# Weight sums made by an adding transfer in six of twenty block-product pairs, with a new table of due times

## The chip, the cores and the metric

The kernel runs on one core of one Trainium2 chip. The metric is the device time of one execution in microseconds (us), as the median of several runs. A core has a matrix engine (TensorE, in the profile PE, with its weight loads shown apart as PEld), a vector engine (VectorE, DVE), a scalar engine (ScalarE, ACT), GpSimd (POOL) and SyncE (SP), which here only issues transfers; 16 DMA engines move the data.

## The reference, cut to what matters

Two decoder layers on 256 tokens of width 1024, float32 throughout. The two mixers differ (block-sparse attention, then a dilated window); after each comes the same MLP, and the change lies in the MLP's second product.

```python
SEQ, D_MODEL, D_FF, DEPTH = 256, 1024, 4096, 2

def sq_relu_mlp(x, w_in, w_out):
    return jnp.square(jax.nn.relu(x @ w_in)) @ w_out

for i in range(DEPTH):
    mix = moba_attention(...) if i % 2 == 0 else dilated_attention(...)
    h = layer_norm(DEEPNORM_ALPHA * h + mix, ...)
    h = layer_norm(DEEPNORM_ALPHA * h + sq_relu_mlp(h, w_in[i], w_out[i]), ...)
```

## The kernel before, in words

**Products.** Each float32 operand is split into a rounded part and a remainder, `hi` and `lo`, and each product is made as three matmuls: hi·hi, hi·lo and lo·hi. All matmuls are written in one helper, line L446 in the profile.

**Weights.** A weight piece of 128x1024 float32 (512 KB) is loaded by SP (L433) into one of 7 buffers named `raw`. ACT rounds it into `whi` (an ACTIVATE, L437), then DVE subtracts to make the remainder `wlo` (L442); `whi` and `wlo` have 10 buffers each, and PE reads them as weights. So each piece passes SP, DMA, ACT, DVE and PE in this order. DVE also copies and adds what comes out of PSUM (`ta`, `tok`, L788 and L795). `acc` and `tp` are PSUM banks.

**Pairs.** A large part of the second MLP product is made in a form of block product with seven multiplications in place of eight. A step of this kind ("pair" here, 10 to a layer, 20 in all) loads two 128x1024 pieces of `w_out`, x and y. With x0, x1 and y0, y1 for their halves of 512 columns, it needs seven weights of 512 columns: from x0 as loaded (w1), from y as loaded (w3, w2), then x0 += x1 and x1 += y0 and a split of the new x (w5, w7), then y0 += x0 and y1 += y0 and a split of the new y (w6, w4). The four sums are DVE tensor_tensor instructions of 128x512 (L788, `raw<-raw,raw` where two buffers or two keys differ, `raw<-raw` within one), 80 in all. `load_duo` writes a pair's loads, sums and splits; `q0` and `q1` are what the other operand becomes for a pair.

**What sets the order.** Nothing is written straight into the program: every operation goes into a planner (`Plan.op`) with its engine, an assumed cost, and what it reads and writes. `order()` gives each one a due time from PE's program order, adds the entry that the table `SHIFT` has for the operation's number, and then lists the operations of each engine by due time as far as buffers and inputs allow. `emit()` writes the program in that order. Each engine then runs its list in order, and waits on semaphores for what comes from others. So an entry of `SHIFT` can move instructions on every engine. SP's loads keep their own order.

**GpSimd** issues no transfer in the kernel before; it has the power step of the layer norm (`rstd`, L1043 and L1048) and a few small things. The adding transfer was already written in `load_duo`, behind a constant, `DMA_SUMS`, that was 0.

Of the kernel before, what the change touches and what calls it, by code (L numbers as in the profile page):

```python
# [12 lines left out]
ALU = mybir.AluOpType  # L13

P = 128
# [121 lines left out]
class Plan:  # L137
# [178 lines left out]
DMA_SUMS = 0.0  # L316
# [60 lines left out]
def tile_trunk(  # L377
# [22 lines left out]
    nc = tc.nc  # L400
    plan = Plan()
    op = plan.op
# [153 lines left out]
    for kt in range(KT):  # L556
        if kt % PER == 0:
            pair = [mk([P, 1024], F32R, t, NSLOT) for t in ("whi", "wlo")]
# [152 lines left out]
    def load_duo(pair, single):  # L711
# [16 lines left out]
        if DMA_SUMS:  # L728
            op(
                "POOL", DMA_SUMS, lambda: nc.gpsimd.dma_start(x.t, pair[:, 512:1536], accum_op=ALU.add), xk, xk,  # L730
                xfer=P * 1024 * 8,
            )
        else:
            tt(512, x0, x0, x1, ALU.add, xk, xk[:1])
            tt(512, x1, x1, y0, ALU.add, xk[1:] + yk[:1], xk[1:])
        w5, w7 = wide(x, 1)
        tt(512, y0, y0, x0, ALU.add, yk[:1] + xk[:1], yk[:1])
# [456 lines left out]
    class Mlp:  # L1194
# [17 lines left out]
        def rest(self, between):  # L1212
# [88 lines left out]
            def do_duo(p):  # L1301
# [4 lines left out]
                q = 1  # L1306
# [372 lines left out]
```

## Time and profile before

| | |
|---|---|
| runs, median (lowest to highest) | 546.93 us (546.81 to 547.24), 3 runs |
| profiled execution: span | 545.7 us, 8666 instructions |
| PE busy | 537.8 us, 3175 matmul records |
| DVE busy | 511.7 us |
| ACT busy | 362.2 us |
| POOL busy | 9.4 us |
| data moved | 105.62 MB, mean 194 GB/s |

The profiled execution has no time of its own beside the span: only the span of its instructions is known, 1.2 us below the median of the runs. The span starts with the first instruction on any engine and ends with the last. Layer 0's MLP lies at about 130 to 285 us, layer 1's at about 375 to 539 us; the pairs lie in both. A row of a table by windows gives the window's length and then, engine by engine, busy microseconds and in brackets the number of instructions; then the granted TensorE clock, the share of the DMA engines that was busy, and GB/s. A row of a timeline gives the start, the busy length, the engine, the line, the operation, output<-inputs and shapes. A row of the waits gives how long was waited in all, how many times, and the longest.

### The profile page before, as it was taken

What the parts mean: (1) busy time and instruction counts of PE and PEld (TensorE: products, weight loads), DVE (VectorE), ACT (ScalarE), POOL (GpSimd) and SP (SyncE); (2) the same over time, 40 slices, a digit from 0 to 9 for tenths busy, and PEclk for the clock granted to TensorE, in tenths of its full rate; (3) what the DMA queues carried; (4) which work ended last, traced back from release to release, by engine and by line L of the source; (5) the groups of instructions that cost most, each with busy time, mean ns of one, the idle gap of its engine ahead of it and who ended that gap; (6) DMA issues with size and microseconds to landing.
All of it is one profiled execution on the core that took longest, in us unless ns stands there. A gap on an engine that the chain in (4) does not pass through costs nothing.

```text
span 545.7 us, 8666 instructions
## 1 busy us (share of the span) xinstructions
PE 537.8 (99%) x3175; PEld 459.4 (84%) x3175; DVE 511.7 (94%) x885; ACT 362.2 (66%) x574; POOL 9.4 (2%) x15
## 2 busy tenths in 40 slices
PE   9999999999999999999999999999999999999994
PEld 7988888888888888888888888888888888888884
DVE  6798999798999999999999999988999999999997
ACT  6558798166958788864843549744877977865720
POOL 0000000000000000000000000000000000000001
PEclk9999999999999999999999999999999999999998
DMA  8985345528626562577845635444843855447502
GB/s 331 406 294 200 116 156 201 224 77 320 221 78 229 201 213 94 193 244 256 287 155 182 267 133 192 153 157 150 295 135 131 283 195 163 155 144 243 191 2 77
DMA packets 30282, 105.62 MB, mean 194 GB/s; under 512 B 3360, under 2 KB 4256, under 8 KB 30240
## 3 DMA queue, kind: packets, MB, share of 16 engines
q1 hardware_dynamic: 28800, 101.46, 53.4%
q10 hardware_dynamic: 1440, 3.61, 2.0%
q8 instruction: 25, 0.41, 0.3%
q14 instruction: 17, 0.14, 0.1%
HBM read 104.01 MB, written 1.05 MB: 193 GB/s over the span
## 4 chain that ended last, share of the span: by engine, by line
PE 84%; DVE 10%; issue 2%; ACT 2%; POOL 0%; DVEq 0%; ACTq 0%; POOLq 0%
PE acc L446 49%; PE tp L446 32%; DVE wlo L442 6%; PE tp L929 3%; DVE raw L788 2%; ACT whi L437 1%; DVE tok L795 1%; DVE ta L788 1%; DVE ta L442 0%; DVE tok L788 0%; POOL rstd L1043 0%; DVE ahi L442 0%; DVE bst L1101 0%; DVEq L1673 0%; ACT ta L1176 0%
## 5 line engine op out<-in xcount | busy, mean ns | idle before, releaser
L437 ACT ACTIVATE whi<-raw 128x1024 fp32r<-128x1024 f32 (+2 forms) x224 | 217.4, 1003 | 81.2 <-PE acc L446 31.2
L442 DVE TENSOR_TENSOR wlo<-raw,whi 128x1024 fp32r<-128x1024 f32 (+2 forms) x226 | 253.3, 1149 | 8.8 <-ACT whi L437 7.0
L446 PE MATMUL acc<-xs,whi 128*128 128x512 f32 (+1 forms) x464 | 107.8, 373 | 0.0
L446 PEld LDWEIGHTS acc<-xs,whi 128*128 128x128 f32 x464 | 81.1, 191 | 14.4 <-ACT xs L437 0.8
L446 PE MATMUL tp<-xs,whi 128*128 128x512 f32 x256 | 63.8, 392 | 0.0
L446 PEld LDWEIGHTS acc<-xs,wlo 128*128 128x128 f32 x416 | 56.9, 191 | 3.5
L446 PE MATMUL acc<-xs,wlo 128*128 128x256 f32 x416 | 59.8, 284 | 0.0
L446 PEld LDWEIGHTS tp<-xs,whi 128*128 128x128 f32 x256 | 46.8, 189 | 8.7
L446 PE MATMUL acc<-whi,ahi 128*128 128x512 f32 (+1 forms) x128 | 47.9, 391 | 0.0
L446 PE MATMUL acc<-wlo,ahi 128*128 128x512 f32 (+1 forms) x108 | 41.7, 386 | 0.0
L446 PEld LDWEIGHTS tp<-xs,wlo 128*128 128x128 f32 x256 | 34.7, 191 | 2.2
L446 PE MATMUL tp<-xs,wlo 128*128 128x256 f32 x256 | 35.6, 283 | 0.0
L446 PE MATMUL acc<-whi,alo 128*128 128x512 f32 (+1 forms) x92 | 33.8, 389 | 0.0
L446 PE MATMUL acc<-whi,xs 128*128 128x512 f32 (+1 forms) x112 | 29.1, 366 | 0.3 <-ACT xs L437 0.3
L788 DVE TENSOR_TENSOR raw<-raw 128x512 f32<-128x512 f32 x40 | 27.4, 688 | 0.6
L788 DVE TENSOR_TENSOR raw<-raw,raw 128x512 f32<-128x512 f32 x40 | 27.5, 688 | 0.5
L446 PEld LDWEIGHTS acc<-whi,ahi 128*128 128x128 f32 x128 | 24.0, 188 | 4.7 <-issue 0.3
L915 ACT ACTIVATE sc<-sc,mx 128x128 f32<-128x128 f32 (+2 forms) x40 | 19.9, 499 | 8.8 <-DVE mx L905 8.5
L446 PE MATMUL tp<-whi,xs 128*128 128x512 f32 x80 | 25.6, 398 | 0.0
L446 PEld LDWEIGHTS acc<-wlo,ahi 128*128 128x128 f32 x108 | 20.4, 188 | 3.7
L446 PEld LDWEIGHTS acc<-whi,xs 128*128 128x128 f32 x112 | 19.9, 189 | 3.8 <-ACT xs L437 0.5
L446 PEld LDWEIGHTS acc<-whi,alo 128*128 128x128 f32 x92 | 17.3, 188 | 3.6
(242 smaller groups left out, 887.0 us busy)
## 6 DMA issues: line engine op xcount, KB each, us to landing
raw<-in_win_dram SPq DMA_DIRECT2D x64, 512.0 KB, 4.3
raw<-in_wout_dram SPq DMA_DIRECT2D x64, 512.0 KB, 4.6
raw<-in_wqk_dram SPq DMA_DIRECT2D x22, 512.0 KB, 5.9
raw<-in_wo_dram SPq DMA_DIRECT2D x14, 512.0 KB, 4.4
raw<-in_wv_dram SPq DMA_DIRECT2D x8, 512.0 KB, 5.6
raw<-in_wv1a_dram SPq DMA_DIRECT2D x4, 512.0 KB, 4.7
tok<-in_xw_dram SPq DMA_DIRECT2D x2, 512.0 KB, 7.1
tok<-in_x_dram SPq DMA_DIRECT2D x2, 512.0 KB, 5.6
```

The source lines that it names most:

```text
L437: op("ACT", act(n, sbuf=sbuf), lambda: nc.scalar.activation(hi(), src(), AF.Copy), r, whi)
L442: lambda: nc.vector.tensor_tensor(lo(), src(), f32(hi()), op=ALU.subtract), list(r) + list(whi), wlo,
L446: nc.tensor.matmul(out_ap, lhsT, rhs, start=start, stop=stop)
L788: op("DVE", dve(n) + extra, lambda: nc.vector.tensor_tensor(out_ap(), a(), b(), op=alu), r, w)
L795: lambda: nc.vector.scalar_tensor_tensor(dst(), a(), s(), b(), op0=o0, op1=o1), r, w,
L915: lambda: nc.scalar.activation(e(), e(), AF.Exp, bias=bias(), scale=-1.0, accum_out=total()), r, w,
L929: nc.tensor.transpose(ps.t[:, c : c + P], src(), ident.t)
```

## The change

In three pairs of each layer (those with index 1, 4 and 7 in the order in which the layer makes them) the two sums x0 += x1 and x1 += y0 are no longer DVE instructions. One transfer that GpSimd issues reads the columns 512 to 1535 of the pair's weights from device memory again, which are x1 and y0 as loaded, and adds them onto x (512 KB read, 128x1024). It must wait until x has landed and both ACT and DVE have read x0 for w1; the split of the new x must wait until it has landed. In layer 1's pair with index 4 the sum y0 += x0 is an adding transfer too, from SBUF to SBUF (256 KB), that must wait for the first one. The table `SHIFT` is replaced as a whole: some 300 entries before, an entry for nearly every operation now. The scratch space for software-built transfers is doubled.

```diff
-DMA_SUMS = 0.0
+DMA_SUMS = 1.0
+ADDED = ({1: 1, 4: 1, 7: 1}, {1: 1, 4: 2, 7: 1})
...
 SHIFT = {
-    178: 5.0, 197: 7.4, 222: 6.2, 229: 27.3, 237: 5.8, 268: -10.9, 276: 15.7, 279: 19.0, 288: 10.5, 308: 29.9, 311:
...
+    0: 1.4, 1: 0.9, 2: -30.7, 3: -23.6, 4: -0.8, 6: -6.8, 8: -4.5, 9: -6.5, 10: -9.7, 11: -6.6, 12: -20.5, 13: 5.8,
...
-    def load_duo(pair, single):
+    def load_duo(pair, single, added):
...
         w3, w2 = wide(y, 0)
-        if DMA_SUMS:
+        if added:
             op(
                 "POOL", DMA_SUMS, lambda: nc.gpsimd.dma_start(x.t, pair[:, 512:1536], accum_op=ALU.add), xk, xk,
                 xfer=P * 1024 * 8,
             )
         else:
             tt(512, x0, x0, x1, ALU.add, xk, xk[:1])
             tt(512, x1, x1, y0, ALU.add, xk[1:] + yk[:1], xk[1:])
         w5, w7 = wide(x, 1)
-        tt(512, y0, y0, x0, ALU.add, yk[:1] + xk[:1], yk[:1])
+        if added == 2:
+            op(
+                "POOL", DMA_SUMS, lambda: nc.gpsimd.dma_start(y0(), x0(), accum_op=ALU.add), yk[:1] + xk[:1], yk[:1],
+                xfer=P * 512 * 8,
+            )
+        else:
+            tt(512, y0, y0, x0, ALU.add, yk[:1] + xk[:1], yk[:1])
         tt(512, y1, y1, y0, ALU.add, yk, yk[1:])
         w6, w4 = wide(y, 2)
...
-                w1, w2, w3, w4, w5, w6, w7 = load_duo(wout[i][p], (*single[0], q))
+                w1, w2, w3, w4, w5, w6, w7 = load_duo(wout[i][p], (*single[0], q), ADDED[i].get(sum(x[0] in 'sS' for x in steps) - 1 - left[0], 0))
...
-    nc = _bacc.Bacc("TRN2", target_bir_lowering=False, num_devices=1, dynamic_dma_scratch_size=256)
+    nc = _bacc.Bacc("TRN2", target_bir_lowering=False, num_devices=1, dynamic_dma_scratch_size=512)
```

Every line number behind the table moves with its new length: L433, L437, L442, L446 and L788 become L718, L722, L727, L731 and L1079; the adding transfers are L1015 and L1024.

How the order moves. PE, ACT and SP have the same instructions as before, DVE has 13 sums fewer, POOL 7 transfers more. SP's list keeps its order. Of PE's some 3130 listed instructions about 2380 stand at another place, by up to 118 places; on DVE the shift reaches 70 places, on ACT 31. The layer norms at the very end stand as before.

The first place is DVE at layer 0's pair with index 4, which lies at about 205 us in the trace of before. x is `raw_503`, y is `raw_504`; w1's remainder goes to `wlo_502`, those of w3/w2, w5/w7 and w6/w4 to `wlo_506`, `wlo_508` and `wlo_510`; `ta`, `g` and `b` rows and `raw_518` belong to other work. Before:

```order
L442 TENSOR_TENSOR wlo_502_2483<-raw_503_2320,whi_501_2469 128x512
L788 TENSOR_TENSOR ta_446_2492<-ta_445_2485 128x256
L788 TENSOR_TENSOR raw_503_2320<-raw_503_2320 128x512
L788 TENSOR_TENSOR raw_503_2320<-raw_503_2320,raw_504_2329 128x512
L442 TENSOR_TENSOR wlo_506_2504<-raw_504_2329,whi_505_2490 128x1024
L788 TENSOR_TENSOR raw_504_2329<-raw_504_2329,raw_503_2320 128x512
L442 TENSOR_TENSOR wlo_508_2524<-raw_503_2320,whi_507_2511 128x1024
L788 TENSOR_TENSOR ta_446_2492<-ta_455_2522 128x256
L788 TENSOR_TENSOR raw_504_2329<-raw_504_2329 128x512
```

After, from the row behind `wlo_502` on:

```order
L1079 TENSOR_TENSOR raw_518_2411<-raw_518_2411 128x512
L1079 TENSOR_TENSOR ta_429_2385<-ta_421_2325,ta_429_2385 128x128
L1079 TENSOR_TENSOR raw_518_2411<-raw_518_2411,raw_519_2451 128x512
L727 TENSOR_TENSOR b_423_2505<-ta_429_2385,b_423_2505 128x384
L1079 TENSOR_TENSOR ta_446_2489<-ta_455_2521 128x256
L727 TENSOR_TENSOR wlo_506_2527<-raw_504_2346,whi_505_2510 128x1024
L1079 TENSOR_TENSOR ta_456_2538<-ta_446_2489 128x128
L1079 TENSOR_TENSOR ta_446_2489<-ta_446_2489 128x128
L1079 TENSOR_TENSOR ta_456_2538<-ta_446_2489,ta_456_2538 128x128 x2
L727 TENSOR_TENSOR q0lo_448_2554<-ta_446_2489,q0hi_447_2547 128x512
L727 TENSOR_TENSOR q1lo_450_2561<-ta_456_2538,q1hi_449_2550 128x384
L1079 TENSOR_TENSOR raw_504_2346<-raw_504_2346,raw_503_2315 128x512
```

The two sums into `raw_503` are gone, and between w1's remainder and the first row that reads the transfer's result, the sum into `raw_504` at the end, now lie twelve instructions (one row stands for two); behind it come the other sum of `raw_504`, a `ta` row of 128x256, and `wlo_508` and `wlo_510`.

On PE at the same pair, where w5 and w7 (`whi_507`, `wlo_508`) are used first. Before, counted from the program's first matmul, the last two rows are its 1377th and 1378th:

```order
L446 MATMUL acc_284_2150<-whi_509_2545,q0lo_448_2580 128x512
L446 MATMUL acc_481_2636<-xs0_1_74,whi_483_2355 128x512 x4
L446 MATMUL acc_481_2636<-xs1_2_75,whi_483_2355 128x512 x4
L446 MATMUL acc_481_2636<-xs0_1_74,wlo_484_2367 128x256 x4
L446 MATMUL acc_481_2636<-xs1_2_75,wlo_484_2367 128x256 x4
L446 MATMUL tp_384_2188<-whi_507_2511,q0hi_447_2570 128x512
L446 MATMUL tp_384_2188<-wlo_508_2524,q0hi_447_2570 128x512
```

After:

```order
L731 MATMUL acc_475_2585<-xs0_1_74,whi_477_2333 128x512
L731 MATMUL acc_475_2585<-xs1_2_75,whi_477_2333 128x512 x2
L731 MATMUL tp_384_2124<-whi_507_2567,q0hi_447_2547 128x512
L731 MATMUL tp_384_2124<-wlo_508_2583,q0hi_447_2547 128x512
L731 MATMUL tp_384_2124<-whi_507_2567,q0lo_448_2554 128x512
L731 MATMUL acc_284_2160<-whi_509_2581,q0hi_447_2547 128x512
L731 MATMUL acc_284_2160<-wlo_510_2594,q0hi_447_2547 128x512
```

The first matmul with `whi_507` (the third row) is the 1348th of the program now, and the first with `wlo_508` the 1349th, 29 places ahead of where they stood; the weights made from y's sums (`whi_509`) now follow, where they came ahead.

The second place is DVE at layer 1's pair with index 4, the one with two transfers: x is `raw_1040`, y is `raw_1041`, and the remainders are `wlo_1039` (w1), `wlo_1043`, `wlo_1045` (w5, w7) and `wlo_1047` (w6, w4). Before:

```order
L442 TENSOR_TENSOR wlo_1039_5191<-raw_1040_5025,whi_1038_5186 128x512
L788 TENSOR_TENSOR ta_983_5199<-ta_982_5179 128x256
L788 TENSOR_TENSOR raw_1040_5025<-raw_1040_5025 128x512
L442 TENSOR_TENSOR wlo_1043_5208<-raw_1041_5035,whi_1042_5193 128x1024
L788 TENSOR_TENSOR raw_1040_5025<-raw_1040_5025,raw_1041_5035 128x512
L788 TENSOR_TENSOR raw_1041_5035<-raw_1041_5035,raw_1040_5025 128x512
L788 TENSOR_TENSOR ta_983_5199<-ta_992_5223 128x256
L788 TENSOR_TENSOR raw_1041_5035<-raw_1041_5035 128x512
L442 TENSOR_TENSOR wlo_1045_5240<-raw_1040_5025,whi_1044_5229 128x1024
L788 TENSOR_TENSOR ta_993_5251<-ta_983_5199 128x128
L788 TENSOR_TENSOR ta_993_5251<-ta_983_5199,ta_993_5251 128x128
```

After, from the fifteenth row behind w1's remainder on:

```order
L1079 TENSOR_TENSOR ta_983_5208<-ta_992_5232 128x256
L727 TENSOR_TENSOR wlo_1045_5249<-raw_1040_5031,whi_1044_5240 128x1024
L1079 TENSOR_TENSOR ta_993_5260<-ta_983_5208 128x128
L1079 TENSOR_TENSOR ta_993_5260<-ta_983_5208,ta_993_5260 128x128
L1079 TENSOR_TENSOR ta_983_5208<-ta_983_5208 128x128
L1079 TENSOR_TENSOR ta_993_5260<-ta_983_5208,ta_993_5260 128x128
L1079 TENSOR_TENSOR ta_999_5273<-ta_998_5266 128x256
L727 TENSOR_TENSOR q0lo_985_5281<-ta_983_5208,q0hi_984_5269 128x512
L1079 TENSOR_TENSOR raw_1041_5046<-raw_1041_5046 128x512
L727 TENSOR_TENSOR q1lo_987_5291<-ta_993_5260,q1hi_986_5278 128x384
L727 TENSOR_TENSOR wlo_1047_5303<-raw_1041_5046,whi_1046_5293 128x1024
L727 TENSOR_TENSOR wlo_1051_5311<-raw_1049_5060,whi_1050_5301 128x1024
```

Three of the four sums are gone, and the whole group, which stood in fourteen rows, is drawn out over 26: w1's remainder stands fifteen rows earlier in DVE's list than before (eight of the fifteen because pairs ahead of it make eight sums fewer), and w6/w4's remainder, `wlo_1047`, is first used by the program's 2807th matmul, where the first was the 2806th before.

The third place is POOL from layer 0's mixer norm to the last mixer norm. Before:

```order
L1048 TENSOR_TENSOR rstd_254_67<-rstd_254_67,expo_3_100 128x1
L1048 TENSOR_TENSOR rstd_276_1529<-rstd_276_1529,expo_3_100 128x1
L1048 TENSOR_TENSOR rstd_611_3190<-rstd_611_3190,expo_3_100 128x1
L1048 TENSOR_TENSOR rstd_630_3235<-rstd_630_3235,expo_3_100 128x1
L1048 TENSOR_TENSOR rstd_791_4173<-rstd_791_4173,expo_3_100 128x1
L1048 TENSOR_TENSOR rstd_813_4230<-rstd_813_4230,expo_3_100 128x1
L1048 TENSOR_TENSOR rstd_1146_5863<-rstd_1146_5863,expo_3_100 128x1
```

After:

```order
L1339 TENSOR_TENSOR rstd_276_1523<-rstd_276_1523,expo_3_100 128x1
L1015 DMA raw_403_1752<-in_wout_dram 128x1024
L1015 DMA raw_503_2315<-in_wout_dram 128x1024
L1015 DMA raw_542_2629<-in_wout_dram 128x1024
L1339 TENSOR_TENSOR rstd_611_3182<-rstd_611_3182,expo_3_100 128x1
L1339 TENSOR_TENSOR rstd_630_3232<-rstd_630_3232,expo_3_100 128x1
L1339 TENSOR_TENSOR rstd_791_4170<-rstd_791_4170,expo_3_100 128x1
L1339 TENSOR_TENSOR rstd_813_4232<-rstd_813_4232,expo_3_100 128x1
L1015 DMA raw_940_4493<-in_wout_dram 128x1024
L1015 DMA raw_1040_5031<-in_wout_dram 128x1024
L1024 DMA raw_1041_5046<-raw_1040_5031 128x512
L1015 DMA raw_1079_5337<-in_wout_dram 128x1024
```

Three transfers stand ahead of layer 0's MLP norm, four ahead of layer 1's; nothing else lies between them on POOL.

342 rows, old and new, of the table SHIFT are left out of this document.

## The prediction

> **What bounds the kernel now.** I read the busy times first, then the chain that ended last, then busy time by stretches, then what PE waited for.
>
> ```profile
> span 545.7 us, 8666 instructions
> PE 537.8 (99%) x3175; PEld 459.4 (84%) x3175; DVE 511.7 (94%) x885; ACT 362.2 (66%) x574; POOL 9.4 (2%) x15
> PE 84%; DVE 10%; issue 2%; ACT 2%; POOL 0%; DVEq 0%; ACTq 0%; POOLq 0%
> ```
>
> PE is busy 99% of the span, DVE 94%, and the chain runs 84% through PE and 10% through DVE. Two engines are thus near full, and the average can't tell which of them holds the other. The stretches can (window, then busy time of PE, PEld, DVE, ACT, POOL):
>
> ```profile
> 0.00:30.00 30.00, 29.23 (x194) 25.97 (x195) 22.25 (x41) 18.99 (x30) 0.94 (x6) 1.00 0.94 363
> 130.00:206.00 76.00, 76.00 (x418) 66.21 (x417) 72.38 (x115) 59.96 (x92) 0.00 (x0) 1.00 0.59 200
> 206.00:285.00 79.00, 79.00 (x372) 66.23 (x371) 78.63 (x116) 53.12 (x68) 0.99 (x1) 1.00 0.62 210
> 285.00:375.00 90.00, 89.75 (x641) 76.71 (x640) 84.52 (x166) 51.81 (x88) 2.76 (x3) 1.00 0.46 166
> 440.00:539.00 99.00, 98.85 (x491) 83.74 (x489) 97.00 (x147) 60.84 (x80) 0.92 (x1) 1.00 0.45 150
> 539.00:545.70 6.70, 0.00 (x0) 0.00 (x0) 3.60 (x7) 0.40 (x1) 1.77 (x2) 0.71 0.23 78
> ```
>
> In the later halves of the two MLPs (206 to 285 and 440 to 539 us) DVE idles 0.37 us of 79 and 2.0 of 99: there it runs level with PE. Yet PE lost nothing in the first and 0.15 us in the second; DVE works off a stock of ready weights and never empties it. Besides these, PE idles 0.77 us at the start and 0.25 at 285, and 6.7 us at the end belong to the last norm, which no row of the change touches. PE's own waits:
>
> ```profile
> PE tp L446 <- PEq L1664: 0.8, 1, 0.8
> PE acc L446 <- ACT xs L437: 0.3, 1, 0.3
> 285.45 0.50 PE L446 MATMUL acc<-whi,xs 128*128 128x512 f32 x1 [0.25 <-ACT xs L437]
> PEld L446 <- issue: 2.4, 7, 0.7
> PEld acc L446 <- ACT xs L437: 1.3, 2, 0.8
> PEld tp L446 <- ACT whi L437: 0.7, 2, 0.4
> ```
>
> One is the program's start, the other lies between the layers. The weight loads' rows below them matter because a matmul's end is modelled: up to 1.3 + 0.7 = 2.0 us of real waiting on ACT may hide in "busy". So PE is the bound nearly throughout, and what it can win by better feeding is 0.4 us visibly and about 2 us at most.
>
> **The change part by part.** PE has the same matmuls in the same shapes: 0 us.
>
> DVE loses 13 sums, seven written `raw<-raw,raw` and six `raw<-raw`:
>
> ```profile
> L788 DVE TENSOR_TENSOR raw<-raw,raw 128x512 f32<-128x512 f32 x40 | 27.5, 688 | 0.5
> L788 DVE TENSOR_TENSOR raw<-raw 128x512 f32<-128x512 f32 x40 | 27.4, 688 | 0.6
> L442 DVE TENSOR_TENSOR wlo<-raw,whi 128x1024 fp32r<-128x1024 f32 x198 | 236.0, 1220 | 8.0 <-ACT whi L437 6.4 <-PE acc L446 0.6
> L437 ACT ACTIVATE whi<-raw 128x1024 fp32r<-128x1024 f32 x198 | 202.8, 1055 | 79.0 <-PE acc L446 30.8 <-DVE raw L788 15.3 <-DVE tok L795 13.5
> ```
>
> 13 x 0.688 = 8.9 us, 4.1 in layer 0 and 4.8 in layer 1. It lies beside PE's matmuls, so its direct worth is only the wait at 285 us, behind the stretch in which DVE was full: -0.25 us, between 0 and -0.5 (that row's whole matmul).
>
> POOL gets seven transfers. None is in the trace of before; the nearest rows are plain loads of the same size, the slowest of that size, and POOL's own arithmetic:
>
> ```profile
> raw<-in_wout_dram SPq DMA_DIRECT2D x64, 512.0 KB, 4.6
> tok<-in_xw_dram SPq DMA_DIRECT2D x2, 512.0 KB, 7.1
> raw<-in_xw_dram SPq DMA_DIRECT2D x3, 256.0 KB, 5.0
> q1 hardware_dynamic: 28800, 101.46, 53.4%
> L1048 POOL TENSOR_TENSOR rstd<-rstd,expo 128x1 f32<-128x1 f32 x7 | 6.6, 950 | 524.7 <-DVE rstd L1046 524.7
> ```
>
> A load of the same bytes lands in 4.6 us: the lower bound, since adding must read x as well. Twice the slowest, 14.2 us, is the upper one. Between them I build an estimate: queue 1 moved 101.46 MB in 53.4% of 545.7 us, so 512 KB cost 291 / 101.46 x 0.524 = 1.5 us of all 16 engines; reading x too costs about that once more, and POOL's making of the transfer about one POOL instruction, 0.95 us. 4.6 + 1.5 + 0.95 = 7.1 us. The 256 KB one I take at its plain row, 5.0 us, since device memory isn't in it.
>
> Where does 7.1 us decide anything? The narrowest single place is layer 0's pair with index 4.
>
> ```profile
> 205.20 0.69 DVE L442 TENSOR_TENSOR wlo<-raw,whi 128x512 fp32r<-128x512 f32 x1
> 206.14 0.68 DVE L788 TENSOR_TENSOR raw<-raw 128x512 f32<-128x512 f32 x1
> 206.86 0.69 DVE L788 TENSOR_TENSOR raw<-raw,raw 128x512 f32<-128x512 f32 x1
> 217.34 0.40 PE L446 MATMUL tp<-whi,q0hi 128*128 128x512 f32 x1
> 222.85 0.40 PE L446 MATMUL tp<-whi,q0hi 128*128 128x512 f32 x1
> ```
>
> w1's remainder ends at 205.89 and may release the transfer; the two sums began 0.25 us later. w5 was used at 222.85. In the new list its remainder meets the program's 1349th matmul, which ran at 217.34 before. Behind the landing DVE has two sums, a 128x256 row (0.42) and the remainder: 2 x 0.69 + 0.42 + 1.22 = 3.0 us. So landing may take 217.34 - 205.89 - 3.0 = 8.4 us (if release and PE keep their distance to one another): 7.1 fits with 1.3 to spare. DVE has twelve instructions to run meanwhile, by their shapes some 6 us, and would then idle 1 us: covered by the two sums that it saved.
>
> The second place is layer 1's pair with index 4, where two transfers follow each other.
>
> ```profile
> 458.70 1.96 DVE L442 TENSOR_TENSOR wlo<-raw,whi 128x1024 fp32r<-128x1024 f32 x2 [0.20 <-ACT whi L437]
> 472.88 0.39 PE L446 MATMUL acc<-whi,q0hi 128*128 128x512 f32 x1
> 473.34 0.39 PE L446 MATMUL acc<-whi,q0lo 128*128 128x512 f32 x1
> ```
>
> w1's remainder (the second of the pair of rows) ended at 460.66. The last weights, `wlo_1047`, now meet the 2807th matmul, at 473.34 in the trace of before. Behind the second landing come one sum, ACT's rounding and the remainder, 0.69 + 1.06 + 1.22 = 3.0 us; that leaves 473.34 - 460.66 - 3.0 = 9.7 us if the release stays where it was. It comes earlier: seven of its fifteen rows are real reordering, at 97.00 / 147 = 0.66 us a row 4.6 us, so up to 14.3 us. The two transfers need 7.1 + 5.0 = 12.1, about the middle of these bounds. I take 0, with +2.4 us as the other end.
>
> The other four pairs have 12 to 22 rows of DVE between release and first reader, 8 to 14 us at 0.66 a row: wide enough at 7.1. The norm on POOL behind each group of transfers stands tens of microseconds after them: 0. SP's list keeps its order, but x keeps its buffer until the split behind the landing, some 6 us longer, and the loads that want one of the seven buffers come later; seven buffers of 512 KB at 210 GB/s turn over in 17 us, so one held 6 us longer delays one load by less than the stock covers: 0 to +1, I take 0. The added traffic, 6.5 x 0.524 = 3.4 MB on 105.6, falls where 45 to 62% of the DMA engines' time is used.
>
> Last the table. About 2380 of 3130 PE rows move. The matmuls cost the same anywhere; what can change is whether each weight and each emptied PSUM bank is there in time. The list after has more places where a remainder stands close ahead of its matmul, and in the stretches from 206 and 440 us a few more than before. One such wait costs 0.3 to 0.4 us by the rows of PE and PEld above; I take one or two, +0.5, between -2.0 (all hidden waits on ACT go) and +2.
>
> Sum on the profiled execution: 545.7 - 0.25 + 0.5 = 545.95, that is no change that matters. The median of the runs lies 1.2 us above that span, and with the same 1.2 the time is 547.1.
>
> **The rivals.** Late transfers (slower): if adding takes not 7.1 but 10 us, layer 0's narrow pair is 1.6 us late on PE, and layer 1's chain 10 + 5 - 12 = 3 us, where 12 is the middle of its two bounds; the rest stay hidden: 547.1 + 4.6 = about 551.5. At the upper bound of 14.2 us it is 5.8 + 7.2 us from these two and a microsecond or two from the other layers' pairs: about 561. It decides from 8.4 + 1.1 = 9.5 us on. For it speaks that no adding transfer was seen and that DMA is 62% busy there; against it, that most loads of the size land in 4.6 us under that same load.
>
> Held-off transfers (slower): DVE is full in just these stretches, and if POOL can build a transfer only while DVE pauses, it is built when DVE stops at the first reader, after some 6 us; then it lands at 6 + 7.1 = 13 us, 4.7 us too late at layer 0's pair, and 3 to 5 us at each of three others: 560 or so. In the trace POOL's rows in DVE's full stretches are only single norms of about 0.95 us, and none shows a stretched one. The Trainium skill ("SBUF — State Buffer", Who interferes with whom) has a rule of this kind: transfers from GpSimd starve while DVE runs in a two-port mode, and two SBUF inputs hamper only a GpSimd instruction that reads. DVE's rows here are mostly of the two-input kind, so by the page's exact wording this rival is unlikely, and no run yet shows it.
>
> Just-in-time order (slower): +0.3 to 0.4 at five or six of the new tight places instead of one or two, 548.5 to 549.
>
> Better feeding (faster): the relief of 8.9 us refills the stock in the two full stretches, and PE loses neither the 0.25 us at 285 nor the hidden waits on ACT: 546.93 - 0.25 - 2.0 = 544.7. Against it: the stock never ran out before.
>
> The sums hidden anyway, nothing else moved: 546.9, which my forecast can't be told from.
>
> **How the numbers follow.** No difference under 0.2%, 1.1 us here, can be told. No measurable change: 0.44, at 547.1 with 546.0 to 548.0 as its own range. Late transfers: 0.20. Held off: 0.06. Just-in-time: 0.12. Better feeding: 0.18, of which nearly all lies between 544.7 and 545.8. So faster 0.18, same 0.44, slower 0.38. The range leaves out the far half of the late transfers and the held-off case above (0.13) and a little of the fast case below (0.06): 545.2 to 551.5.
>
> **What would show it.** Right: PE at 537 to 539 us busy, no PE wait on whi or ta above 1 us, DVE's busy time down to about 503, the adding transfers landing 6 to 8 us from issue, the last norm still 6.7 us long. Wrong: landings above 9.5 us with DVE idle ahead of `raw<-raw,raw` or ACT ahead of `whi` on the transfer, and PE gaps near 217 or 472 us; gaps elsewhere would be the table's; a shorter PE stretch from the first matmul to the last with no transfer late would be better feeding.

## The result: 0.5% slower, and the profile after

| | before | after |
|---|---|---|
| median of the runs | 547.09 us (546.81 to 547.61, 4 runs) | 550.18 us (549.89 to 550.46, 4 runs) |
| ratio after to before | | 1.0053, 95% interval 1.0038 to 1.0067 |
| profiled execution: span | 545.7 us | 548.2 us (time 550.44) |
| start of the last matmul | 538.57 us | 540.49 us |

One execution of the kernel before (1387 us, beside e1 to e4) and one of e4 (782 us) lie far outside all others and are left out of every ratio.

The page of the changed kernel, its first lines and its list of waits on PE:

```profile
span 548.2 us, 8686 instructions
PE 539.0 (98%) x3175; PEld 458.3 (84%) x3175; DVE 505.8 (92%) x872; ACT 362.4 (66%) x574; POOL 15.0 (3%) x22
PE 90%; DVE 6%; DMA 2%; issue 1%; ACT 0%; DVEq 0%; SPq 0%; POOL 0%
```

```profile
PE tp L731 <- PEq L1955: 0.8, 1, 0.8
PE acc L731 <- ACT ta L1555: 0.7, 1, 0.7
PE tp L1220 <- DVE tok L1086: 0.2, 1, 0.2
```

PE is the bound as before: the chain runs 90% through it, and DVE got lighter. The old wait at 285 us on ACT's `xs` is gone; a wait on ACT's `ta` has come, 0.7 us, on the matmuls of L731 that write `acc`. The stretches say where (columns as in the prediction):

```profile
206.00:285.00 79.00, 79.00 (x370) 65.94 (x368) 77.03 (x113) 52.24 (x67) 2.78 (x3) 1.00 0.69 223
440.00:541.00 101.00, 100.08 (x497) 84.53 (x495) 95.31 (x145) 61.39 (x81) 3.57 (x4) 1.00 0.51 154
541.00:548.20 7.20, 0.00 (x0) 0.00 (x0) 3.52 (x7) 0.40 (x1) 1.01 (x2) 0.76 0.40 146
```

DVE's idle time grew in both of its full stretches, from 0.37 us to 1.97 of 79, and from 2.0 of 99 to 5.7 of 101. PE made nothing of it: in the last stretch it idles 0.92 us where it idled 0.15. This is the timeline there, in layer 1's pair with index 4:

```profile
466.81 1.98 PE L731 MATMUL acc<-xs,whi 128*128 128x512 f32 x8
468.62 1.11 PE L731 MATMUL acc<-xs,wlo 128*128 128x256 f32 x8
469.77 0.60 ACT L1555 ACTIVATE ta<-acc 128x512 f32<-128x512 f32 x1 [1.42 <-PE acc L731]
470.42 0.97 PE L731 MATMUL acc<-xs,whi 128*128 128x512 f32 x3 [0.69 <-ACT ta L1555]
```

Three of the four `acc` banks hold running sums of the MLP's second product here; one, the working bank, is left to make the other operand, product after product (988, 994, 1012 in the list). The 16 matmuls of product 994 end at 469.7, ACT empties the bank until 470.4, and only then can 1012 begin. Before, six matmuls on other banks stood between these two products, the first and the last of them in the two middle rows here (1012 begins in the last row); in the new list there are none.

```profile
465.82 1.00 PE L446 MATMUL acc<-xs,wlo 128*128 128x256 f32 x7
466.66 0.40 PE L446 MATMUL tp<-whi,sc 128*128 128x512 f32 x1
467.82 0.39 PE L446 MATMUL acc<-whi,v 128*128 128x512 f32 x1
468.05 1.98 PE L446 MATMUL acc<-xs,whi 128*128 128x512 f32 x8
```

The transfers did what was asked of them (start, busy time, engine, operation; in brackets POOL's idle time and what ended it):

```profile
207.83 0.90 POOL L1015 DMA_DIRECT2D raw<-in_wout_dram  x1 [53.14 <-DVE raw L1079]
458.51 0.88 POOL L1015 DMA_DIRECT2D raw<-in_wout_dram  x1 [51.51 <-DVE wlo L727]
466.45 0.89 POOL L1024 DMA_DIRECT2D raw<-raw  x1 [7.06 <-DMA raw<-in_wout_dram]
raw<-in_wout_dram SPq DMA_DIRECT2D x64, 512.0 KB, 4.9
raw<-in_wout_dram POOLq DMA_DIRECT2D x6, 512.0 KB, 5.7
raw<-raw POOLq DMA_DIRECT2D x1, 256.0 KB, 3.2
```

0.9 us on POOL, and 5.7 us from issue to landing, in which the POOL row is counted; the small one 3.2 us. One by one, four of the six landed in 5.5 to 5.7 us and two, of layer 1, in 7.1 and 7.3.

Put together, the last matmul starts 1.92 us later. Part of that is the start of the execution: in e11 (below) PE has the same list as in the changed kernel, yet its traced execution is 0.7 us ahead from 13 us on and stays so to the last matmul, 539.78 against 540.49. The last group of norm transposes of layer 0's mixer (PE's rows `tp<-ident,tok` at 118.7 us before and 119.1 after) is a mark behind which this no longer counts. From the mark to the last matmul PE takes 419.85 to 419.88 us in three traces with the old list (before, e2, e9) and 421.39 to 421.46 in three with the new one (after, e11, e6): 1.5 us more. Against each shape's usual pitch, PE lost 0.95 us of it at 469 us (the 0.69 of the row and the slow restart behind it); the other 0.6 us is spread, 0.3 of it over the stretch from the mark to 292 us. The stretch from the last matmul to the end of the span is 0.58 us longer (6.85 and 7.43 us), and the time lies 2.2 us above the span, where the kernel before lies 1.8 above it (its executions beside the experiments with the least change, below). 1.92 + 0.58 + 0.45 = 2.95 us is what lies between these two executions; the medians are 3.1 us apart.

### The profile page after: what moved, and what is told of

It reads as the page before. It is cut to its first block, busy times and chain, and to the rows that moved or that the text cites. A ratio compares the mean times of both kernels' runs of the same rounds, so it can differ in the third digit from the quotient of the medians.

```text
span 548.2 us, 8686 instructions
## 1 busy us (share of the span) xinstructions
PE 539.0 (98%) x3175; PEld 458.3 (84%) x3175; DVE 505.8 (92%) x872; ACT 362.4 (66%) x574; POOL 15.0 (3%) x22
## 4 chain that ended last, share of the span: by engine, by line
PE 90%; DVE 6%; DMA 2%; issue 1%; ACT 0%; DVEq 0%; SPq 0%; POOL 0%
PE acc L731 54%; PE tp L731 34%; PE tp L1220 3%; DVE tok L1086 2%; DVE wlo L727 2%; DMA g<-in_xw_dram 1%; DMA raw<-in_xw_dram 1%; DVE bst L1392 0%; DVE ta L727 0%; DVE tok L1079 0%; DVE bst L1362 0%; ACT whi L722 0%; DVE ta L1079 0%; ACT ta L1555 0%; DVE mv L1332 0%
## 5 line engine op out<-in xcount | busy, mean ns | idle before, releaser
L722 ACT ACTIVATE whi<-raw 128x1024 fp32r<-128x1024 f32 (+2 forms) x224 | 217.5, 1003 | 83.4 <-PE acc L731 24.0
L727 DVE TENSOR_TENSOR wlo<-raw,whi 128x1024 fp32r<-128x1024 f32 (+2 forms) x226 | 252.2, 1147 | 7.8 <-ACT whi L722 6.4
L731 PE MATMUL acc<-xs,whi 128*128 128x512 f32 (+1 forms) x464 | 110.7, 372 | 0.8 <-ACT ta L1555 0.7
L731 PEld LDWEIGHTS acc<-xs,whi 128*128 128x128 f32 x464 | 81.1, 190 | 15.7 <-ACT ta L1555 0.9
L731 PE MATMUL tp<-xs,whi 128*128 128x512 f32 x256 | 66.1, 393 | 0.0
L731 PE MATMUL acc<-xs,wlo 128*128 128x256 f32 x416 | 62.0, 283 | 0.0
L731 PEld LDWEIGHTS acc<-xs,wlo 128*128 128x128 f32 x416 | 58.1, 190 | 3.9
L731 PEld LDWEIGHTS tp<-xs,whi 128*128 128x128 f32 x256 | 46.0, 188 | 8.3 <-DVE ta L1079 0.2
L731 PE MATMUL acc<-whi,ahi 128*128 128x512 f32 (+1 forms) x128 | 48.0, 388 | 0.0
L731 PE MATMUL acc<-wlo,ahi 128*128 128x512 f32 (+1 forms) x108 | 41.7, 386 | 0.0
L731 PEld LDWEIGHTS tp<-xs,wlo 128*128 128x128 f32 x256 | 36.0, 190 | 2.9
L731 PE MATMUL tp<-xs,wlo 128*128 128x256 f32 x256 | 37.4, 282 | 0.0
L731 PE MATMUL acc<-whi,alo 128*128 128x512 f32 (+1 forms) x92 | 33.7, 388 | 0.0
L731 PE MATMUL acc<-whi,xs 128*128 128x512 f32 (+1 forms) x112 | 29.7, 369 | 0.0
L731 PEld LDWEIGHTS acc<-whi,ahi 128*128 128x128 f32 x128 | 24.0, 188 | 4.8 <-issue 0.3
L731 PE MATMUL tp<-whi,xs 128*128 128x512 f32 x80 | 25.6, 397 | 0.0
L1079 DVE TENSOR_TENSOR raw<-raw 128x512 f32<-128x512 f32 x34 | 23.3, 687 | 0.5
L731 PEld LDWEIGHTS acc<-wlo,ahi 128*128 128x128 f32 x108 | 20.3, 188 | 3.8
L1079 DVE TENSOR_TENSOR raw<-raw,raw 128x512 f32<-128x512 f32 x33 | 22.7, 688 | 0.7
L1206 ACT ACTIVATE sc<-sc,mx 128x256 f32<-128x256 f32 (+2 forms) x40 | 19.9, 499 | 5.2 <-DVE mx L1196 5.0
L731 PEld LDWEIGHTS acc<-whi,xs 128*128 128x128 f32 x112 | 19.6, 189 | 3.5 <-issue 0.3
L1079 DVE TENSOR_TENSOR ta<-ta 128x128 f32<-128x128 f32 (+1 forms) x48 | 15.9, 330 | 5.4 <-ACT ta L1555 4.1
```

Source lines behind the costliest of these rows:

```text
L722: op("ACT", act(n, sbuf=sbuf), lambda: nc.scalar.activation(hi(), src(), AF.Copy), r, whi)
L727: lambda: nc.vector.tensor_tensor(lo(), src(), f32(hi()), op=ALU.subtract), list(r) + list(whi), wlo,
L731: nc.tensor.matmul(out_ap, lhsT, rhs, start=start, stop=stop)
L1079: op("DVE", dve(n) + extra, lambda: nc.vector.tensor_tensor(out_ap(), a(), b(), op=alu), r, w)
L1206: lambda: nc.scalar.activation(e(), e(), AF.Exp, bias=bias(), scale=-1.0, accum_out=total()), r, w,
```

## The experiments

Theory A: the new order costs. Theory B: the transfers cost, by the time or traffic that they take. Theory C: a kernel with any software-built transfer pays outside its span. The runs of each group share the runs of the kernel before, and a ratio is to those.

**Order kept, sums back on DVE (e1).** The program in the changed kernel's order, with the 13 sums where POOL issued the transfers:

```diff
-"POOL", DMA_SUMS, lambda: nc.gpsimd.dma_start(x.t, pair[:, 512:1536], accum_op=ALU.add), xk, xk,
+"POOL", DMA_SUMS, lambda: (nc.vector.tensor_tensor(x0(), x0(), x1(), op=ALU.add), nc.vector.tensor_tensor(x1(), x1(), y0(), op=ALU.add)), xk, xk,
```

> The changed kernel's program in exactly its order, but the seven transfers are put back as the 13 sums on DVE, written at the places where POOL issued the transfers. Theory A (the new order costs: the wait of PE at 469 us, 0.9 us, small waits elsewhere, 0.5 us in the last stores): span stays near 548, the PE wait near 469 us stays, time 549 to 550. Theory B (the transfers cost, by sharing the DMA engines or by work outside the span): span 546 and time about 547. Theory C (half outside the span, from having software transfers at all): span 547.5 to 548, time about 549, that is 1.1 us less than the changed kernel outside the span.

Measured: 555.4 us, ratio 1.015 (1.0137 to 1.0163), span 553.7. Its waits on PE:

```profile
PE acc L731 <- ACT ta L1555: 2.0, 4, 0.7
PE tp L731 <- DVE ta L1079: 1.1, 2, 0.7
PE acc L731 <- DVE alo L727: 0.6, 1, 0.6
```

No theory had this number. The new order without the transfers is 8.1 us slower than the kernel before (547.3 beside it); with them it is 3.1 slower. So in this order the 8.9 us of sums are worth some 5 us, and the order itself leans on a DVE without them. The wait between the products 994 and 1012 is there too, in a program without any transfer, so it belongs to the order:

```profile
475.18 1.89 PE L731 MATMUL acc<-xs,whi 128*128 128x512 f32 x7 [0.69 <-ACT ta L1555]
```

B's 547 did not come, but e1 puts 8.9 us of work back on DVE and so gives no price of the transfers; that is left to e9.

**One small software transfer (e2).** The kernel before with 8 KB more, issued by POOL, read by nobody:

```diff
+spare_t = mk([P, 16], F32, "extra", 1)
+late.fn = lambda: (pow_fn(), nc.gpsimd.dma_start(spare_t.t, ident_in[:, :16]))
```

> The kernel before with one more transfer issued by GpSimd at its third instruction of the norm, 128x16 float32 (8 KB) into a tile that nobody reads. Theory C (a kernel with any software transfer pays some 1.1 us outside its span): span 545.7 as before, time 548.1. Theories A and B: time 547.0 to 547.2, no difference from before.

Measured: 547.27 us against 547.35, ratio 1.0001 (0.9992 to 1.0009), span 545.7. C falls as far as one transfer goes (for six see e9). The time lies 1.8 us above the span here, in all eleven executions 1.73 to 1.82.

**Transfers with the old table (e3), the new table without transfers (e4).** Only the table, or only `ADDED`, is exchanged, with the operations' numbers carried over.

> The transfers alone: the changed kernel with the table of due times of the kernel before, its numbers moved to the same operations (the two entries of sums that no longer exist fall away); the planner orders anew. Theory A: no wait of PE near 469 us, span 545.5 to 546.5; with theory C 548 outside, without it 547. Theory B: span 547 to 548, time 549 to 550.

> The table alone: the kernel before with the new table, numbers moved to the same operations (no entry for the sums that take the transfers' place); the planner orders anew. Theory A: span 547 to 549, time 548.5 to 550. Theory B: span 546 and time about 547.

Measured: e3 566.97 us, ratio 1.0371 (1.0348 to 1.0394); e4 569.4 to 572.1 us in four executions, ratio 1.0424 (1.0407 to 1.044). Both expectations missed by some 20 us. The planner orders anew after each change, and here a table made for one list of operations did not serve another: in e3 PE waited on remainders (4.0 and 2.2 us) and on ACT's `ta` (3.1), in e4 on ACT's `ta` (8.3). The two don't split the change into a part of the table and a part of the transfers; for that the order has to be held, as in e1 and e9.

**The bank's wait, first try (e5).** Twelve matmuls ahead of the products in the shared bank are dealt out 5, 5, 4, 4 instead of 6, 6, 6 and none (by operation and part: behind which operation what now stands):

```diff
+moved = {3046: ((3217, 2), (3218, 0), (3218, 1), (3218, 2), (3213, 0)),
+         3067: ((3213, 1), (3213, 2), (3219, 0), (3219, 1)),
+         3098: ((3219, 2), (3214, 0), (3214, 1), (3214, 2))}
```

> The changed kernel with one edit of PE's list near 469 us: the twelve matmuls on other banks that stood, six and six and none, between the products that share one PSUM bank (988, 994 and 1012, with six ahead of 988) are dealt out as 5, 5, 4 and 4, so that none of these products follows the one before it at once. Theory A1 (PE waits there because the bank must first be emptied by ACT): the wait of 0.7 to 0.9 us goes, span 547.3 to 547.5, time 0.7 to 0.9 us under the changed kernel, about 549.4. Rival A2 (the wait is the late transfer's, PE has nothing to do before w5): the wait moves on to the matmuls with w5 some microseconds later, span 548.2, time as the changed kernel, 550.2.

Measured: 550.73 us, ratio 1.0065 (1.0053 to 1.0077), span 548.0. Neither: the wait came earlier, not later. ACT, then PE, in its timeline:

```profile
459.71 1.06 ACT L740 ACTIVATE whi<-raw 128x1024 fp32r<-128x1024 f32 x1 [2.37 <-PE acc L749]
462.13 0.58 ACT L1578 ACTIVATE ta<-acc 128x512 f32<-128x512 f32 x1
462.76 2.11 PE L749 MATMUL acc<-xs,whi 128*128 128x512 f32 x8 [0.97 <-ACT ta L1578]
```

This `whi` (1042) takes the weight buffer of `whi_1034` in the changed kernel and starts at 458.70. In e5 one of the moved matmuls is the last to read `whi_1034`, so that the row is given the buffer of `whi_980` instead, and waits until PE's products with it are done, at 459.7. (The buffers are read from the program; the trace shows that the row waits for PE's `acc` products here and for a `tp` matmul in the changed kernel.) Behind it in ACT's list stands the emptying of the same bank for an earlier product, 462.13 instead of 461.47, and with one matmul less for cover there PE waited 0.97 us. The gap at 469 was closed, and another opened.

**The bank's wait, second try (e10).** Three matmuls that are ready, into another bank (operation 3266), are put between 994 and 1012; no buffer comes free later by it:

```diff
+if o.n != 3266:
+    out.append(o)
+if o.n == 3098:
+    out.append(by[3266])
```

> The changed kernel with one edit of PE's list: three matmuls into bank tp_920 with weights whi_1038 and the operand g, which are ready by 462 us, go from behind the pair's first products to between product 994 and product 1012, where PE waited for the working bank; no weight buffer comes free later by it. Theory A1 (the bank's emptying by ACT is what PE waits for): 0.69 us of the 0.85 us are covered, the wait at 470 falls to 0.2 or goes, time 0.6 to 0.7 under the changed kernel, about 549.5, against a late w5, w6 or q0 taking its place: 550.0 to 550.2.

Measured: 549.37 us, ratio 1.0041 (1.0027 to 1.0055), span 547.7.

```profile
469.64 0.40 PE L743 MATMUL tp<-whi,g 128*128 128x512 f32 x1
469.88 0.40 PE L743 MATMUL tp<-wlo,g 128*128 128x512 f32 x1
470.11 0.39 PE L743 MATMUL tp<-whi,g 128*128 128x512 f32 x1
470.49 1.19 PE L743 MATMUL acc<-xs,whi 128*128 128x512 f32 x4
```

The wait is gone from PE's list, as A1 said: of the 0.95 us lost there, 0.26 are left. The median lies 0.8 us under the changed kernel's, but the intervals of the two ratios overlap, and executions of both kernels come about 0.6 us apart (549.3 and 550.0 here, 549.9 and 550.45 there), so 0.4 to 0.6 us is what like with like gives. From the mark at 118 us to the last matmul the trace has 421.04 us against 421.39, and that of e12, with the same edit, 420.78. So the trace shows the cause of that wait, and the times its size only to within some tenths.

**The tail (e6, e7, e12).** The last norms' rows on DVE in the order of the kernel before: alone, with e5's edit, and with e10's.

```diff
+if o.n == 3444:
+    out.append(by[3441])
+if o.n == 3475:
+    out.append(by[3476])
+if o.n == 3482:
+    out.append(by[3484])
```

> The changed kernel with the last norms' rows on DVE in the order of the kernel before (second half of the first block's output right behind its first half; 768 columns ahead of 256; both pieces of 384 ahead of the 128). PE is untouched. If the tail's order costs: the stretch behind the last matmul falls from 7.4 to 6.9 us, span 547.7, time about 549.7. If the longer tail is chance between executions: no change, 550.2.

> Both edits, of the bank and of the tail. Theory A (order costs that add up): 0.85 + 0.5 = 1.3 us under the changed kernel, span 546.8 to 547.0, time 548.8. If the bank's wait is only moved: 549.7.

> The edit of the ready matmuls and the edit of the tail's order together. The tail's order alone measured 549.76 against 550.18 in another group of runs, but beside the bank's edit it gave nothing. If both add up: 549.0 to 549.2; if the tail is worth nothing: as the ready matmuls alone. It stays above the kernel before in any case, since 1 us of small waits and 0.5 us outside the span are untouched.

Measured: e6 549.76 us (ratio 1.0049, 1.0037 to 1.0062), e7 550.71 (1.0062, 1.005 to 1.0074; e5 beside it 550.73), e12 549.43 (1.004, 1.0028 to 1.0053; e10 beside it 549.37). Behind the last matmul the spans have 7.2 to 7.3 us with the edit and 7.4 without, so it returns 0.1 to 0.2 of the 0.58 us in the traces and nothing that the times can show. The traces tell where the rest is. Of the stores to `out_dram`, first of before, then of after:

```profile
L1059 ACTq DMA_DIRECT2D out_dram<-tok x2: 350/352/353, 542.1 to 542.7; - x2
DMA to landing us min/median/max: 1.8/2.0/2.1
L1350 ACTq DMA_DIRECT2D out_dram<-tok x2: 354/412/471, 544.2 to 544.6; - x2
DMA to landing us min/median/max: 1.6/2.0/2.3
```

The last store lands 6.14 us behind the last matmul's start before and 6.38 after. e1 has 6.37, so these 0.24 us are the order's; e6 has 6.29, with ACT's two stores still the other way round than before. From that landing to the end of the span it is 0.99 us before and 1.32 after, and that goes with the transfers by POOL: 0.93 and 0.94 without any (e4, e1), 1.11 with one (e2), 1.25 with three and with six (e8, e9), 1.32 with seven (e3 has 1.61, with one longer pause of 0.4 near its end). In this stretch SP works off the semaphores of the transfers, 0.06 us a row: three such rows stand behind the last landing before, two in e1, eight after. So 0.24 + 0.33 is the whole tail.

**Transfers in the old order (e8).** Each operation is due at its start in the plan of the kernel before, and three pairs have their first two sums as a transfer:

```diff
-self.ops[n].due += shift
+o.due = DUE[o.n]
-ADDED = ({1: 1, 4: 1, 7: 1}, {1: 1, 4: 2, 7: 1})
+ADDED = ({1: 1, 4: 1}, {1: 1})
```

> Transfers in the old order: each operation's due time is the start that it had in the plan of the kernel before, and three pairs only have their two sums as a transfer (index 1 and 4 of layer 0, index 1 of layer 1), those whose results are used late enough there. PE's list is that of before but for 36 places of at most 6. Theory A (the transfers themselves cost PE nothing where there is room): span 545.5 to 546.2, time 547.0 to 547.7. Theory B (each transfer costs some 0.4 us of PE or DMA time wherever it stands): 548.3 or more. If the six sums that DVE saves here were worth time: below 546.5.

Measured: 549.87 us, ratio 1.0047 (1.0034 to 1.006), span 548.1. That is B's number, but not by B's way. At layer 0's pair with index 4 the timeline has

```profile
206.40 0.89 POOL L1176 DMA_DIRECT2D raw<-in_wout_dram  x1 [54.53 <-DVE ta L1240]
213.66 1.04 ACT L883 ACTIVATE whi<-raw 128x1024 fp32r<-128x1024 f32 x1
214.61 0.58 ACT L1716 ACTIVATE ta<-acc 128x512 f32<-128x512 f32 x1
215.24 0.50 PE L892 MATMUL acc<-xs,whi 128*128 128x512 f32 x1 [0.36 <-ACT ta L1716]
```

ACT rounds the transfer's result as soon as it has landed, and the emptying of the working bank stands behind that row; PE waits for it, 0.5 us. The others lie far from any transfer: 0.8 us more at 285, where PE waits on ACT's `xs` (0.9 us in two waits), and 0.5 at 369 us. DVE's list differs from that of before in rows of the norms there too. So e8 shows one way in which a transfer costs through the order, and no clean price of transfers.

**The transfers alone (e9).** The kernel before in its own order with all its sums, and six adding transfers of the same size beside them, onto device memory that nobody reads:

```diff
+first.fn = lambda f=first.fn, pair=pair, extra=extra, x=x: (
+    f(), nc.gpsimd.tensor_copy(warm.t[:, 0:1], x.t[:, 0:1]),
+    nc.gpsimd.dma_start(extra, pair[:, 512:1536], accum_op=ALU.add),
+)
```

> The kernel before in its own order, all sums on DVE, and beside them six adding transfers of 512 KB by GpSimd, each issued behind the first sum of the six pairs (POOL copies one column of x first, which makes it wait for that sum). They add the same 512 KB of weights onto scratch in device memory that nobody reads, so no instruction waits for them. This prices the transfers alone: POOL's work, the DMA engines' time, and what lies outside the span. If transfers cost nothing beside the waits for them (theory A): span 545.7 to 546.0, time 547.0 to 547.4. If they slow the loads, DVE or the end of the program (theory B): 548 or more; the part outside the span shows whether the changed kernel's 2.3 us there, against 1.8 of the kernel before, is theirs.

Measured: 547.44 us against 547.2, ratio 1.0003 (0.9994 to 1.0012).

```profile
span 545.3 us, 8689 instructions
PE 537.5 (99%) x3175; PEld 458.3 (84%) x3175; DVE 511.3 (94%) x885; ACT 362.2 (66%) x574; POOL 21.3 (4%) x27
extra<-in_wout_dram POOLq DMA_DIRECT2D x6, 512.0 KB, 5.8
```

Six transfers that nobody waits for cost PE nothing: from the mark at 118 us to the last matmul it takes 419.88 us, and 419.87 before. What they cost lies at the end: 0.26 us more from the last landing to the end of the span, as told above, and outside the span 1.86 to 1.95 us in eleven executions against 1.74 to 1.81 in the fifteen of the kernel before beside them. The times can't resolve this sum of 0.4 us. The transfers end in device memory here and not in SBUF, so the write into SBUF is left out of this price.

**The second transfer undone (e11).** y0 += x0 of layer 1's pair with index 4 back on DVE, in the changed kernel's order:

```diff
-"POOL", DMA_SUMS, lambda: nc.gpsimd.dma_start(y0(), x0(), accum_op=ALU.add), yk[:1] + xk[:1], yk[:1],
+"POOL", DMA_SUMS, lambda: nc.vector.tensor_tensor(y0(), y0(), x0(), op=ALU.add), yk[:1] + xk[:1], yk[:1],
```

> The changed kernel in its order with only the second transfer of layer 1's pair of index 4 undone: y0 += x0 is a DVE sum again, written where POOL issued the transfer. The second transfer took 0.9 us on POOL and landed in 3.2, the sum takes 0.69. DVE's list gets a row that waits for the first transfer, some 3 us ahead of rows that don't need it. If DVE held behind that row costs PE: 550.5 to 552. If the later landing of the chain was a cost in the changed kernel: 549.5 or less. If neither: 550.2.

Measured: 549.74 us, ratio 1.0048 (1.0035 to 1.0061), not told apart from the changed kernel's 1.0053; the wait of 0.7 us on ACT's `ta` stays, and from the mark at 118 us to the last matmul both traces have 421.39 us. The chain of two transfers cost PE nothing.

No version beat the kernel before; e10 and e12 are the nearest, 2.2 us above it.

## Why the prediction was right, and where its working failed

550.18 lies in the forecast range of 545.2 to 551.5, with slower at 0.38, but the likeliest case was no measurable change at 547.1, and none of its slower rivals is what happened as it was told. That the range held the time is luck: its upper end was made for late transfers, and no wait of PE stands behind a transfer. Three of its sums are off: 547.1 + 4.6 is 551.7, the held-off rival's own terms give 561 to 567 and not 560, and half of 0.20 with 0.06 is 0.16 and not 0.13.

*PE bounds the kernel, and DVE's relief is off its path:* right, by the chain and by DVE's idle time. The two groups of sums fell by the forecast 8.9 us:

```profile
L1079 DVE TENSOR_TENSOR raw<-raw 128x512 f32<-128x512 f32 x34 | 23.3, 687 | 0.5
L1079 DVE TENSOR_TENSOR raw<-raw,raw 128x512 f32<-128x512 f32 x33 | 22.7, 688 | 0.7
```

54.9 to 46.0. DVE's busy time fell by 5.9 only, to 505.8 and not 503: rows that run back to back overlap by almost 0.1 us in the profile, a shared stretch counts once, and the rows overlap less where DVE has pauses (the rows' lengths add up to 568.3 us before and 558.5 after, 9.8 less). The wait at 285 on `xs` went, as forecast.

*The transfer's price, 7.1 us, and 5.0 for the small one:* 5.7 us with POOL's 0.9 in it, and 3.2 likewise. Of the estimate's parts POOL's 0.95 us and the plain load's 4.6 held; the 1.5 us for reading x too did not show in four of the six, which landed 4.6 to 4.7 us behind the end of their POOL row. The two in layer 1 took 7.1 and 7.3 in all, near the estimate.

*The narrow pair, 1.3 us to spare:* both ends came 1.1 to 1.3 us later and the distance held.

```profile
206.54 0.68 DVE L727 TENSOR_TENSOR wlo<-raw,whi 128x512 fp32r<-128x512 f32 x1
214.39 0.69 DVE L1079 TENSOR_TENSOR raw<-raw,raw 128x512 f32<-128x512 f32 x1
216.06 2.35 DVE L727 TENSOR_TENSOR wlo<-raw,whi 128x1024 fp32r<-128x1024 f32 x2
218.48 0.39 PE L731 MATMUL tp<-wlo,q0hi 128*128 128x512 f32 x1
```

`wlo_508`, the first of the two in the third row, ended at 217.3 and was used at 218.48: 1.2 us to spare. The chain of two transfers fits as well, by e11. So the rival of late transfers had its mechanism refuted, though its time, 551.5, is not far from what was measured.

*Held-off transfers:* refuted. POOL's rows lasted 0.88 to 1.02 us and landings 5.5 to 7.3, not 13, in stretches where DVE is busy 91 to 98%. By the Trainium skill ("SBUF — State Buffer", Who interferes with whom) a DVE instruction with two SBUF inputs contends with a GpSimd instruction that reads SBUF, not with one that only writes it. The trace agrees in so far as no POOL row of a transfer was stretched.

*The table, +0.5 us as one or two waits of 0.3 to 0.4:* this is the step that failed. The term was +1.9 us on PE between the two traces, 1.5 of them free of the start. Of these, 0.95 us is one wait at a place that I had not priced, since I asked only whether weights are there in time. I named emptied banks as a condition in one sentence, and then counted none. The rest is small pieces, which the runs don't resolve.

*"The last norm, which no row of the change touches", 0 us:* wrong, and so is the sentence in the part on the change that the norms at the end stand as before. PE's and POOL's rows there do; on DVE the second half of the first block's output had moved ten rows back, and its stores with it, and ACT's last two stores had changed places. The tail grew by 0.58 us: 0.24 from the order, and 0.33 because SP has the semaphores of seven more transfers to work off at the end, a term that the prediction did not have.

*1.2 us between span and time:* 1.8 for the kernel before by e2, 2.2 to 2.4 for the changed one; the traced execution of before thus took about 547.5 us and not the median. What the 0.5 us are is open. The transfers alone bring 0.1 of them (e9 1.9, e3 1.85), the new order alone none (e1 1.8), while e4, without a transfer, has 2.2.

So shown are: the wait at 469, its cause (e10) and that it is the order's (e1); that traffic and making of the transfers cost PE nothing (e9), and the end of the program, in the span and outside it, some 0.4 us; and that they are worth some 5 us in the order that was made around them (e1). About 0.6 us on PE in small pieces, the start, and 0.4 us outside the span stay unexplained.

## What to carry to other kernels

Taking work off an engine that is busy but hardly ever waited for bought nothing here, and the new order that made room for it cost more than it returned: hold the order fixed and change the work alone, then the work fixed and the order alone, before blaming either. Where all buffers of a kind are in use, look for the place where two products follow each other in the same PSUM bank with nothing between them; the engine that empties the bank is then on the path. When small differences between traces are read, first find how far executions of the same list differ at their start. And a table of due times belongs to one list of operations: with 13 sums exchanged for 7 transfers, or back, it cost some 20 us (e3, e4).

## What the runs showed of the hardware

An adding transfer of 512 KB from device memory landed in 5.7 us (median of six, 5.5 to 7.3) where a plain load of that size took 4.9 in the same kernel (median of 64, 3.5 to 9.0), both from the start of the issuing row. That row lasts 0.9 us on POOL and 0.33 on SP; from its end it is 4.6 to 4.7 us for four of the six, and 4.5 for the plain load's median. So in these four the adding itself shows as 0.1 to 0.2 us, and most of the difference is the longer issue. The Trainium skill ("DMA: Bandwidth & Descriptors", Anatomy of one DMA — SWDGE (gpsimd) path) gives 2.0 us + bytes / 436e3, an estimate of 3.2 us for 512 KB and 4.4 for twice that. The measured 5.5 to 7.3 lies above both, with the DMA engines 51 to 72% busy with other loads around it.
